# Hybrid trunk on one core: all three branch products walk token tile by token tile, the second tile's inputs are finished late, and the skip multiply of the state space branch changes engine

## The chip, the cores and the metric

The kernel runs on one core of one Trainium2 chip. The time is device microseconds of one execution; several runs are taken and their median is given. A profiled execution has a time of its own and a span, from its first to its last instruction.

## What is computed

Two layers over 256 tokens of 1024 channels. A layer is a feed-forward block, a mixer and a second feed-forward block. Only the mixer is touched. From the reference:

```python
q, k, v, z, xbc, dt_raw, u, vg, gate_raw = jnp.split(xn @ w_in, split_at, axis=-1)
y_a = moba_attention(q, k, v)                        # 8 heads of 128, causal, ALiBi
xbc = jax.nn.silu(causal_depthwise_conv(xbc, conv_w, conv_b))
xs, bm, cm = jnp.split(xbc, ...)
y_s = ssd_scan(xs, dt, a, bm, cm) + d_skip[:, None] * xs     # the skip: d_skip * xs
y_s = rms_norm(y_s * jax.nn.silu(z), ssm_norm_g)
y_c = u * sv                                         # gated unit from u and vg
merged = gates[0]*(y_a @ p_attn) + gates[1]*(y_s @ p_ssm) + gates[2]*(y_c @ p_sgu)
return merged @ w_out
```

## The kernel before, in words

The 256 tokens are two token tiles of 128 (t = 0 and 1); TensorE (PE) multiplies them by weights that arrive as blocks of 128 x 1024 (`raw`, one 512 KB DMA each, issued on SyncE's queue, SP). Every product is taken in split precision: ScalarE (ACT) casts a block to `whi` (L180), VectorE (DVE) subtracts to get `wlo` (L181), and PE runs three matmuls of 512 columns for each unit of 128 input channels: `whi`, `wlo` with the high part of the activations, `whi` with the low part (L213, L214, L215). A block serves two units of each token tile. Eleven split blocks (`SPLIT`) and six raw ones (`RAW`) can be held.

The order of every engine's instructions is written by the program itself. Side work is a Python generator, a task: `spawn` puts it on a list, and after each unit `pump(0.65)` lets 0.65 of planned time pass and steps those whose delay is over. `yield W["pv"]` means that the task goes on 13.0 planned units later; `finish(task)` steps it to its end at once. So the delays in the table `W` decide between which units of a weight product the instructions of a task are written, and each engine runs its own list in that order.

`gemm(..., tail=8)` takes the last eight blocks by token tile: all 16 units of t = 0 (48 matmuls), then all 16 of t = 1. With `tail=0` the tiles alternate, two units of one and two of the other.

The mixer's order is: projections xbc, z, q, k, v; meanwhile the state space task `ssd`; then for each branch its gate projection and its branch product `br`. Branch 0 is the state space branch (input `ysx`), branch 1 attention (`yax`), branch 2 the gated unit (`ycx`, which already has `tail=8`). Between branches 0 and 1 stands the projection vg.

The names that the argument uses:
- `ssd`: for each tile t and group g (of 2), PE makes `seg` (L707), DVE and ACT turn it into weights `ssw` (L709, L713 on ACT, L715; two halves), PE multiplies them with `xs` into `yd` (L738, two halves of eight matmuls), and for t = 1 also `yo` (L744). DVE adds `yd` to `y` (L741), which frees one of the three psum slots `tr` for the next `seg`; then L746, L748, L749. The skip product (L695) puts d_skip * xs into `y` before that. L698 scales `xs` by dt in place.
- `y` is then transposed through memory (L277 on DVE, `turn<-y` and `y<-turn` on SP) and split into `ysh` and `ysl` (ACT L674, DVE L675), the inputs of branch 0; `yt` holds one such task for each tile.
- `qtok` transposes (L277) belong to the q and k tiles.
- `attention`: scores `qk` (L798), DVE adds the position term into `sc` (L802), maximum (L807), `nmx` (L809), exponentials on ACT (L814), division (L820), transposes through memory (L277, `turn<-sc` x8, then `sc<-turn` x2), and `W["pv"]` later the products `pv` (L837) on PE, whose results are split into `yah` and `yal` for branch 1.
- `merge` (L916 and below): DVE multiplies a finished `br` tile by its gate.

Of the kernel before, what the change touches and what calls it, by code (L numbers as in the profile page):

```python
# [16 lines left out]
P = 128  # L17
# [7 lines left out]
NH = 8  # L25
# [26 lines left out]
def trunk(ctx, tc, a):  # L52
# [31 lines left out]
    def tr(name):  # L84
        return psum.tile([P, 512], F32, name=name, tag="tr", bufs=TR)

    def small(name, n, dt=F32, bufs=2):
        return sm.tile([P, n], dt, name=name, tag=name, bufs=bufs)
# [187 lines left out]
    def turn(src, m, e=128):  # L276
        V.transpose(src, src)  # L277
        rd = dram.tile([m, 4, 32, 4, e], F32, name=f"turn{m}_{e}", tag=f"turn{m}_{e}", bufs=8)
        for b in range(4):
            nc.sync.dma_start(rd[:, :, :, b, :].rearrange("m c i e -> i (m c) e"),  # L280
                              src[32 * b:32 * b + 32].rearrange("p (x e) -> p x e", e=e))
        return rd

    def land(dst, rd):
        nc.sync.dma_start(dst, rd.rearrange("m c i a e -> (c i) m (a e)"))
# [202 lines left out]
    def mixer(l, x, r2, nxt):  # L488
# [189 lines left out]
        def ssd(ysx, rs):  # L678
# [13 lines left out]
            def scaled(t):  # L692

                y[t] = b4(f"y{t}")
                G.tensor_tensor(h3(y[t]), h3(xs[t]), hpar[:, l, 2, :, None].to_broadcast([P, SH, SP]),  # L695
                                op=ALU.mult)
                xdt[t] = xs[t]
                V.tensor_tensor(h3(xdt[t]), h3(xs[t]),  # L698
                                st["dt"][:, t * SH:(t + 1) * SH, None].to_broadcast([P, SH, SP]), op=ALU.mult)
# [19 lines left out]
            for t in range(NT):  # L719
                for g in range(SG):  # L720
                    weights(t, 2 * g)
                    if t == 0:
                        scaled(g)
                    yield W["w1"]
                    weights(t, 2 * g + 1)
                    if t == 0:

                        pst = tr("state")
                        T.matmul(pst, bc["b"][:, g * P:(g + 1) * P], xw[:, 512 * g:512 * g + 512],
                                 start=True, stop=True)  # L730
                        A.copy(state[:, 512 * g:512 * g + 512], pst)
                    yield W["w2"]
                    c = slice(512 * g, 512 * g + 512)
                    py = tr("yd")
                    for q in (2 * g, 2 * g + 1):
                        for j in range(4):
                            hh = q * 4 + j
                            T.matmul(py[:, (hh - 8 * g) * SP:(hh - 8 * g + 1) * SP], ws[t, q][:, j, :],  # L738
                                     xdt[t][:, hh * SP:(hh + 1) * SP], start=True, stop=True)
                        ws.pop((t, q))  # L740
                    V.tensor_tensor(y[t][:, c], py, y[t][:, c], op=ALU.add)  # L741
                    if t == 1:
                        po = tr("yo")
                        T.matmul(po, cT(g, 1), state[:, c], start=True, stop=True)  # L744
                        tmp = b2("yo")
                        V.tensor_tensor(h3(tmp, 8), h3(po, 8),  # L746
                                        st["eac"][:, 8 * g:8 * g + 8, None].to_broadcast([P, 8, SP]), op=ALU.mult)
                        V.tensor_tensor(y[t][:, c], y[t][:, c], tmp, op=ALU.add)  # L748
                    V.tensor_tensor(y[t][:, c], y[t][:, c], zs[t][:, c], op=ALU.mult)  # L749
                rs[t] = rsqrt([sumsq(y[t], "sy")], "rs", 1.0 / D)  # L750
                yt[t] = spawn(turned(t, y[t], pl[:, G_SSM:G_SSM + 8]), wait=1.3 if t else 6.5)
# [26 lines left out]
                A.activation(vv[t][:, 512 * c:512 * c + 512], ps[t], AF.Copy, scale=r2[t])  # L778
            yield W["vv"]

        def attention(yax, free):
            for t in range(NT):
                while t and not free:
                    yield 0

                m = t + 1
                n = m * P
                per = 512 // n
                sc, s4 = {}, {}
                mx = small("mx", NH)  # L790
                for g in range(2):
                    sc[g] = (b4 if t else b2)("sc", (P, 4 * n))
                    s4[g] = sc[g].rearrange("p (b h j) -> p h b j", h=4, j=32)
                    for u in range(0, 4, per):
                        ps = tr("qk")
                        for j in range(per):
                            hh = u + j
                            T.matmul(ps[:, j * n:(j + 1) * n], qk["q", g][:, hh, t * P:(t + 1) * P],  # L798
                                     qk["k", g][:, hh, 0:n // 32], start=True, stop=True)
                        for j in range(per):  # L800
                            hh = u + j
                            V.scalar_tensor_tensor(s4[g][:, hh], alibi[t].rearrange("p (b j) -> p b j", j=32),  # L802
                                                   2.0 ** -(4 * g + hh + 1),
                                                   ps[:, j * n:(j + 1) * n].rearrange("p (b j) -> p b j", j=32),
                                                   op0=ALU.mult, op1=ALU.add)
                        yield W["qs"]
                    V.tensor_reduce(mx[:, 4 * g:4 * g + 4], s4[g], axis=AX.XY, op=ALU.max)  # L807
                nmx = small("nmx", NH)
                V.tensor_scalar(nmx, mx, -1.0, None, op0=ALU.mult)  # L809
                den = small("den", NH)  # L810
                for g in range(2):
                    for j in range(4):
                        c = slice(4 * g + j, 4 * g + j + 1)
                        A.activation(s4[g][:, j], s4[g][:, j], AF.Exp, bias=nmx[:, c], accum_out=den[:, c])  # L814
                    yield W["ex"]
                rden = small("rden", NH)
                V.reciprocal(rden, den)
                rd = {}
                for g in range(2):
                    V.tensor_tensor(sc[g].rearrange("p (b h j) -> p b h j", h=4, j=32),  # L820
                                    sc[g].rearrange("p (b h j) -> p b h j", h=4, j=32),
                                    rden[:, None, 4 * g:4 * g + 4, None].to_broadcast([P, 4 * m, 4, 32]), op=ALU.mult)
                    rd[g] = turn(sc[g], m)
                    yield 1.3
                yield W["so"]
                for g in range(2):
                    land(sc[g].rearrange("p (m e) -> p m e", m=m), rd[g])
                yield W["pv"]
                hi, lo = yax.new(t)
                for g in range(2):  # L830

                    pts = sc[g].rearrange("p (m a h j) -> p m h a j", m=m, a=4, h=4)
                    po = tr("pv")
                    for j in range(4):
                        hh = 4 * g + j
                        for k in range(t + 1):
                            T.matmul(po[:, j * P:(j + 1) * P], vv[k][:, hh * HD:(hh + 1) * HD], pts[:, k, j],  # L837
                                     start=k == 0, stop=k == t)
                    halves(po, hi[:, 4 * g:4 * g + 4, :], lo[:, 4 * g:4 * g + 4, :])
                    yield 1.3  # L840


        uu, vg = {}, {}
# [78 lines left out]
                yield W["mg"]  # L922
                yield from to_parts(merged[t], *then.new(t))

        def branch(bx, rs, need, first=False, then=None):
            store = {}
            es = []
            for c in range(2):
                [ps] = project("gate")
                es.append(spawn(gate_evac(store, c, ps, rs)))  # L930
            finish(*need)
            finish(*es)
            slots, dst = accs("br")
            ready, out = set(), {}

            def on_done(key, t):
                ready.add((key, t))
                if t not in out:
                    out[t] = spawn(merge(t, slots, ready, store, first, then))

            gemm(chunk(0) + chunk(1), bx.h, bx.l, dst, tail=8 if then is not None else 0, on_done=on_done)
            return out

        ysx, yax, ycx, mx = XT("ys"), XT("ya"), XT("yc"), XT("mg")
# [17 lines left out]
        finish(ss)  # L962
        finish(*at)
        free = []
        att = spawn(attention(yax, free))
        b0 = branch(ysx, rs, [ss, *yt.values()], first=True)
        free.append(True)
        gl = []
        for c in range(2):
            gl.append(spawn(gelu_evac(vg, "vg", c, project("vg")[0])))  # L970
        b1 = branch(yax, None, [att, *b0.values()])
        gw = spawn(spatial_weights(l))
        finish(*gl)
        gl = [spawn(gelu_evac(uu, "u", 0, project("u")[0]))]
# [204 lines left out]
```

## Time and profile before

| | |
|---|---|
| median of 3 runs | 1488.76 us (1488.53 to 1488.9) |
| profiled execution, its own time | 1487.31 us |
| profiled execution, span | 1485.5 us |
| outside the span | 1.81 us |
| PE busy | 1458.3 us, 98% of the span |
| DVE, ACT, GpSimd (POOL) busy | 970.1, 767.6, 57.0 us |
| granted TensorE clock, mean | 0.997 |

The profiled execution lies 1.45 us below the median. A time in a row is counted from the start of the span; an instruction's duration includes overlap with the next one, so the distance between two starts says what it costs. What stands in brackets behind a row is the idle time of the engine ahead of it and what ended it.

### The profile page before, as it was taken

How to read it: one execution, taken by the hardware profiler on the slowest of the kernel's cores; microseconds unless marked ns; L12 is line 12 of the kernel's file. 1: busy time of each engine (PE TensorE's matmuls, PEld its weight loads, DVE VectorE, ACT ScalarE, POOL GpSimd, SP SyncE). 2: the span in 40 equal slices, each digit the busy share in tenths (PEclk: the TensorE clock that was granted, in tenths of full speed). 3: DMA queues.
4: the chain of work that ended last, by engine and by line, in shares of the span. 5: the costliest groups of instructions: out<-in, count | busy, mean ns of one | idle time of the engine just before them, and what ended most of it. 6: DMA issues, size and time to landing. Idle time of an engine off the chain costs nothing.

```text
span 1485.5 us, 18564 instructions
## 1 busy us (share of the span) xinstructions
PE 1458.3 (98%) x6706; PEld 1204.4 (81%) x6706; DVE 970.1 (65%) x1188; ACT 767.6 (52%) x1051; POOL 57.0 (4%) x98
## 2 busy tenths in 40 slices
PE   9999999999989999999999999999999899999998
PEld 6888888777878888888888888888778788888886
DVE  6766477777666857666486564876776667676652
ACT  6544367555464537544364443765553644464441
POOL 0000021000000001000000000210000000000000
PEclk9999999999999999999999999999999999999999
DMA  8977655577567445877458874656774765477860
GB/s 291 333 227 255 198 185 183 156 201 246 190 216 228 167 155 197 284 242 255 154 193 281 252 254 128 217 169 172 250 230 155 232 206 170 136 265 245 260 200 28
DMA packets 151003, 312.23 MB, mean 210 GB/s; under 512 B 35456, under 2 KB 76544, under 8 KB 150912
## 3 DMA queue, kind: packets, MB, share of 16 engines
q1 hardware_dynamic: 150336, 310.73, 64.6%
q8 instruction: 52, 0.85, 0.2%
q10 hardware_dynamic: 576, 0.33, 0.1%
q14 instruction: 39, 0.32, 0.1%
HBM read 288.98 MB, written 22.02 MB: 209 GB/s over the span
## 4 chain that ended last, share of the span: by engine, by line
PE 61%; DVE 9%; ACT 3%; DMA 3%; issue 2%; POOL 0%; SPq 0%; DVEq 0%; ACTq 0%; POOLq 0%
PE gu L213 8%; PE gu L215 8%; PE gu L214 8%; DVE wlo L181 5%; PE dn L213 4%; PE dn L215 4%; PE dn L214 4%; PE br L213 3%; PE br L215 3%; PE br L214 3%; ACT whi L180 1%; PE wo L213 1%; PE wo L215 1%; PE u L215 1%; PE u L214 1%
## 5 line engine op out<-in xcount | busy, mean ns | idle before, releaser
L181 DVE TENSOR_TENSOR wlo<-raw,whi 128x1024 fp32r<-128x1024 f32 x495 | 595.3, 1225 | 330.1 <-ACT whi L180 329.5
L180 ACT CAST whi<-raw 128x1024 fp32r<-128x1024 f32 x495 | 512.3, 1051 | 404.5 <-PE gu L215 162.8
L213 PE MATMUL gu<-whi,xh 128*128 128x512 f32 x704 | 276.0, 392 | 1.9 <-ACT xh L328 1.5
L214 PE MATMUL gu<-wlo,xh 128*128 128x512 f32 x704 | 274.9, 390 | 0.0
L215 PE MATMUL gu<-whi,xl 128*128 128x512 f32 x704 | 274.6, 390 | 0.0
L213 PEld LDWEIGHTS gu<-whi,xh 128*128 128x128 f32 x704 | 132.5, 188 | 30.2 <-ACT xh L328 2.0
L215 PEld LDWEIGHTS gu<-whi,xl 128*128 128x128 f32 x704 | 132.5, 188 | 28.2 <-DVE xl L329 0.6
L214 PEld LDWEIGHTS gu<-wlo,xh 128*128 128x128 f32 x704 | 132.5, 188 | 28.2 <-DVE wlo L169 0.9
L213 PE MATMUL dn<-whi,hTh 128*128 128x512 f32 x352 | 137.5, 391 | 0.0
L215 PE MATMUL dn<-whi,hTl 128*128 128x512 f32 x352 | 137.0, 389 | 0.0
L214 PE MATMUL dn<-wlo,hTh 128*128 128x512 f32 x352 | 136.9, 389 | 0.0
L215 PEld LDWEIGHTS dn<-whi,hTl 128*128 128x128 f32 x352 | 66.1, 188 | 13.9
L214 PEld LDWEIGHTS dn<-wlo,hTh 128*128 128x128 f32 x352 | 66.1, 188 | 13.5
L213 PEld LDWEIGHTS dn<-whi,hTh 128*128 128x128 f32 x352 | 66.1, 188 | 13.3
L213 PE MATMUL gate<-whi,xh 128*128 128x512 f32 x192 | 76.6, 399 | 0.0
L215 PE MATMUL gate<-whi,xl 128*128 128x512 f32 x192 | 74.9, 390 | 0.0
L214 PE MATMUL gate<-wlo,xh 128*128 128x512 f32 x192 | 74.8, 389 | 0.0
L328 ACT CAST xh<-xg 128x512 fp32r<-128x512 f32 (+1 forms) x25 | 15.1, 603 | 62.1 <-DVE xg L326 62.1
L713 ACT ACTIVATE ssw<-ssw,nacs 128x128 f32<-128x128 f32 x64 | 20.5, 390 | 49.6 <-DVE ssw L709 49.6
L215 PEld LDWEIGHTS gate<-whi,xl 128*128 128x128 f32 x192 | 36.0, 188 | 7.7
L214 PEld LDWEIGHTS gate<-wlo,xh 128*128 128x128 f32 x192 | 36.1, 188 | 6.9
L417 ACT ACTIVATE silu<-gu,r 128x512 f32<-128x512 f32 (+1 forms) x48 | 31.4, 654 | 19.9 <-PE gu L215 16.2
(239 smaller groups left out, 2229.3 us busy)
## 6 DMA issues: line engine op xcount, KB each, us to landing
raw<-in_mix SPq DMA_DIRECT2D x232, 512.0 KB, 4.4
raw<-in_gu SPq DMA_DIRECT2D x175, 512.0 KB, 4.9
raw<-in_dn SPq DMA_DIRECT2D x88, 512.0 KB, 4.5
turn<-hh SPq DMA_DIRECT2D x160, 64.0 KB, 1.8
hh<-turn SPq DMA_DIRECT2D x40, 256.0 KB, 5.3
row_ffn_post_g<-in_ffn_post_g SPq DMA_DIRECT2D x4, 512.0 KB, 5.2
turnw<-qtok SPq DMA_DIRECT2D x32, 64.0 KB, 2.6
qT<-turnw SPq DMA_DIRECT2D x4, 512.0 KB, 6.1
```

The costliest lines, as they stand in the source:

```text
L180: A.copy(hi, w)
L181: V.tensor_tensor(lo, w, hi.bitcast(F32), op=ALU.subtract)
L213: T.matmul(o, xh(k, t), hi[:, off:off + n], start=first, stop=False)
L214: T.matmul(o, xh(k, t), lo[:, off:off + n], start=False, stop=False)
L215: T.matmul(o, xl(k, t), hi[:, off:off + n], start=False, stop=last)
L328: A.copy(o_h, xg)
L417: A.activation(silu[t][:, :w], gate(t), AF.Silu, scale=r2[t])
L713: A.activation(w[:, j, :], w[:, j, :], AF.Exp, bias=st["nacs"][:, c:c + 1])
```

## The change

Four edits. The skip product L695 is taken by DVE, where GpSimd took it. The delay ahead of the second half of a group in `ssd` grows by 1.3 planned units for t = 1. `attention` becomes one task for each tile, and its delay ahead of `pv` grows from 13.0 to 19.5 for t = 1. `branch` always uses `tail=8`, and can finish the tasks of a tile (`late`) when the product first asks for that tile, instead of finishing all of them ahead of the product: branch 0 does so with `yt`, branch 1 with the attention tasks. (The body of `attention` is otherwise only indented less and is cut here.)

```diff
-                G.tensor_tensor(h3(y[t]), h3(xs[t]), hpar[:, l, 2, :, None].to_broadcast([P, SH, SP]),
+                V.tensor_tensor(h3(y[t]), h3(xs[t]), hpar[:, l, 2, :, None].to_broadcast([P, SH, SP]),
                                 op=ALU.mult)
...
-                    yield W["w2"]
+                    yield W["w2"] + 1.3 * t
...
-        def attention(yax, free):
-            for t in range(NT):
-                while t and not free:
-                    yield 0
+        def attention(t, yax, free):
+            while t and not free:
+                yield 0
...
-                yield W["pv"]
+            yield W["pv"] + 6.5 * t
...
-        def branch(bx, rs, need, first=False, then=None):
+        def branch(bx, rs, need, late=None, first=False, then=None):
...
-            gemm(chunk(0) + chunk(1), bx.h, bx.l, dst, tail=8 if then is not None else 0, on_done=on_done)
+
+            if late is not None:
+                bx = guarded(bx, gate_on(late, finish))
+            gemm(chunk(0) + chunk(1), bx.h, bx.l, dst, tail=8, on_done=on_done)
...
-        att = spawn(attention(yax, free))
-        b0 = branch(ysx, rs, [ss, *yt.values()], first=True)
+        att = {t: spawn(attention(t, yax, free)) for t in range(NT)}
+        b0 = branch(ysx, rs, [ss], yt, first=True)
+        finish(att[0])
         free.append(True)
...
-        b1 = branch(yax, None, [att, *b0.values()])
+        b1 = branch(yax, None, [*b0.values()], att)
```

The helper that finishes a tile's task when the product first asks for it was there before:

```python
def gate_on(tail, finish):
    seen = set()
    def wait(k, t):
        if t not in seen:
            finish(tail[t])
            seen.add(t)
    return wait
```

How instructions move, in layer 1 (layer 2 moves in the same way). First DVE, in the state space task of tile 1 (`y_2583`) while the v projection runs on PE; the transposes of a k tile (`qtok`) are the row that moves:

```order
 L277 STREAM_TRANSPOSE y_2468<-y_2468 128x1024
 L181 TENSOR_TENSOR wlo<-raw,whi 128x1024
+L277 STREAM_TRANSPOSE qtok<-qtok 128x512 x2
 L741 TENSOR_TENSOR y_2583<-yd,y_2583 128x512
 L746 TENSOR_TENSOR yo<-yo,eac 128x512
```

They now stand ahead of the L741 that frees the psum slot; before they stood six rows further on, behind the next L715. The two skip products stand on DVE directly ahead of each L698, and a group's `yd` of tile 1 is written six matmuls later on PE (group 0) and twelve later (group 1).

Second PE, the start of branch product 0 (`ysh_3023`, `ysl_3024` are tile 0, `ysh_3198` and `ysl_3199` tile 1):

```order
-L213 MATMUL br<-whi,ysh_3198 128x512
-L214 MATMUL br<-wlo,ysh_3198 128x512
-L215 MATMUL br<-whi,ysl_3199 128x512
-L213 MATMUL br<-whi,ysh_3198 128x512
-L214 MATMUL br<-wlo,ysh_3198 128x512
-L215 MATMUL br<-whi,ysl_3199 128x512
 L213 MATMUL br<-whi,ysh_3023 128x512
 L214 MATMUL br<-wlo,ysh_3023 128x512
```

The units of tile 1 are gone from between those of tile 0: 48 matmuls of tile 0 now stand ahead of the first of tile 1, where six did. The `pv` of attention tile 0 keeps its place, 24 matmuls behind the start of the product.

Third PE, the first `pv` of attention tile 1, inside the gate projection of branch 1 (`xh0`, `xh1` are the two token tiles, the number behind `whi` is that of the block). Before it stood ahead of block 3456:

```order
L837 MATMUL pv_3714<-sc_3438,v1_2928 128x128
L213 MATMUL gate_3648<-whi_3456,xh0_1595 128x512
L214 MATMUL gate_3648<-wlo_3457,xh0_1595 128x512
```

Now it stands ahead of the second tile's units of block 3516:

```order
L836 MATMUL pv_3768<-sc_3438,v1_2928 128x128
L213 MATMUL gate_3747<-whi_3516,xh1_1682 128x512
L214 MATMUL gate_3747<-wlo_3517,xh1_1682 128x512
```

That is 30 matmuls of 512 columns later. On SP the read `y<-turn` of tile 1 stands behind one more `raw` load than before; no other load of the mixer passes another.

## Rows read from the trace of the kernel before

**Rows 1.** Head of the page: the span, and PE's busy time.
```profile
span 1485.5 us, 18564 instructions
PE 1458.3 (98%) x6706; PEld 1204.4 (81%) x6706; DVE 970.1 (65%) x1188; ACT 767.6 (52%) x1051; POOL 57.0 (4%) x98
```

**Rows 2.** Waits of PE, whole execution: releaser, us in total, times, longest.
```profile
PE pv L837 <- DMA sc<-turn: 8.3, 2, 4.2
PE yd L738 <- DVE ssw L715: 4.7, 4, 1.4
PE br L213 <- ACT ysh L674: 3.1, 2, 1.6
```

**Rows 3.** PE in order of time, layer 1, state space task beside the v projection.
```profile
301.04 1.89 PE L738 MATMUL yd<-xs,ssw 128*128 128x64 f32 x16
...
314.19 1.00 PE L738 MATMUL yd<-xs,ssw 128*128 128x64 f32 x8
316.64 1.10 PE L738 MATMUL yd<-xs,ssw 128*128 128x64 f32 x8 [1.45 <-DVE ssw L715]
...
322.10 0.50 PE L707 MATMUL seg<-acsr,sel 128*128 128x512 f32 x1 [0.47 <-DVE y L741]
...
332.50 1.10 PE L738 MATMUL yd<-xs,ssw 128*128 128x64 f32 x8 [0.90 <-DVE ssw L715]
```

**Rows 4.** PE in order of time, layer 1, branch product 0.
```profile
365.72 0.39 PE L214 MATMUL br<-wlo,ysh 128*128 128x512 f32 x1
365.95 0.39 PE L215 MATMUL br<-whi,ysl 128*128 128x512 f32 x1
367.88 0.50 PE L213 MATMUL br<-whi,ysh 128*128 128x512 f32 x1 [1.55 <-ACT ysh L674]
...
372.37 1.05 PE L837 MATMUL pv<-sc,v 128*128 128x128 f32 x8
```

**Rows 5.** PE in order of time, layer 1, the two pv sets of attention tile 1.
```profile
428.28 3.50 PE L837 MATMUL pv<-sc,v 128*128 128x128 f32 x16 [4.09 <-DMA sc<-turn]
...
433.01 1.95 PE L837 MATMUL pv<-sc,v 128*128 128x128 f32 x16
```

**Rows 6.** Stretches: PE, PEld, DVE, ACT, POOL busy, granted clock, DMA share, GB/s.
```profile
240.00:290.00 50.00, 50.00 (x269) 41.42 (x268) 32.92 (x56) 29.45 (x46) 4.41 (x2) 1.00 0.56 168
...
415.00:440.00 25.00, 20.91 (x102) 17.88 (x101) 18.11 (x20) 16.79 (x23) 0.00 (x0) 0.93 0.79 250
```

**Rows 7.** GpSimd (POOL) in order of time, 240 to 260 us.
```profile
248.16 1.91 POOL L695 TENSOR_TENSOR y<-xs,hpar 128x1024 f32<-128x1024 f32 x1 [25.54 <-DMA raw<-in_mix]
250.41 2.50 POOL L695 TENSOR_TENSOR y<-xs,hpar 128x1024 f32<-128x1024 f32 x1 [0.35 <-ACT xs L563]
```

**Rows 8.** DVE in order of time, layer 1, state space task.
```profile
290.02 1.23 DVE L181 TENSOR_TENSOR wlo<-raw,whi 128x1024 fp32r<-128x1024 f32 x1 [2.65 <-ACT whi L180]
...
295.12 1.22 DVE L698 TENSOR_TENSOR xs<-xs,dt 128x1024 f32<-128x1024 f32 x1
...
300.61 0.69 DVE L715 TENSOR_TENSOR ssw<-ssw,cbt 128x512 f32<-128x512 f32 x1 [1.35 <-ACT ssw L713]
...
321.37 0.68 DVE L741 TENSOR_TENSOR y<-yd,y 128x512 f32<-128x512 f32 x1
...
327.34 1.30 DVE L277 STREAM_TRANSPOSE qtok<-qtok 128x512 f32<-128x512 f32 x2
...
331.75 0.69 DVE L715 TENSOR_TENSOR ssw<-ssw,cbt 128x512 f32<-128x512 f32 x1 [1.41 <-ACT ssw L713]
```

**Rows 9.** SP's DMA issues in order of time, layer 1.
```profile
365.91 0.89 SPq L285 DMA_DIRECT2D sc<-turn  x2
...
423.61 0.93 SPq L285 DMA_DIRECT2D sc<-turn  x2
```

**Rows 10.** DMA issues of 340 to 440 us: KB each, median us to landing.
```profile
sc<-turn SPq DMA_DIRECT2D x2, 256.0 KB, 5.2
```

**Rows 11.** DVE in order of time, layer 1, the merges of branch product 0.
```profile
389.15 1.29 DVE L916 TENSOR_TENSOR merged<-br,gate 128x512 f32<-128x512 f32 x2 [9.46 <-PE br L214]
```

More of the change, by code (lines that the diff above doesn't have):

```diff
@@ L779, in v_evac @@
             yield W["vv"]
-        def attention(yax, free):
-            for t in range(NT):
-                while t and not free:
-                    yield 0
[L786 to L827, printed above, removed]
-                yield W["pv"]
[L829 to L840, printed above, removed]
@@ new lines, in attention @@
+        def attention(t, yax, free):
+            while t and not free:
+                yield 0
+            m = t + 1
+            n = m * P
+            per = 512 // n
+            sc, s4 = {}, {}
+            mx = small("mx", NH)
+            for g in range(2):
+                sc[g] = (b4 if t else b2)("sc", (P, 4 * n))
+                s4[g] = sc[g].rearrange("p (b h j) -> p h b j", h=4, j=32)
+                for u in range(0, 4, per):
+                    ps = tr("qk")
+                    for j in range(per):
+                        hh = u + j
+                        T.matmul(ps[:, j * n:(j + 1) * n], qk["q", g][:, hh, t * P:(t + 1) * P],
+                                 qk["k", g][:, hh, 0:n // 32], start=True, stop=True)
+                    for j in range(per):
+                        hh = u + j
+                        V.scalar_tensor_tensor(s4[g][:, hh], alibi[t].rearrange("p (b j) -> p b j", j=32),
+                                               2.0 ** -(4 * g + hh + 1),
+                                               ps[:, j * n:(j + 1) * n].rearrange("p (b j) -> p b j", j=32),
+                                               op0=ALU.mult, op1=ALU.add)
+                    yield W["qs"]
+                V.tensor_reduce(mx[:, 4 * g:4 * g + 4], s4[g], axis=AX.XY, op=ALU.max)
+            nmx = small("nmx", NH)
+            V.tensor_scalar(nmx, mx, -1.0, None, op0=ALU.mult)
+            den = small("den", NH)
+            for g in range(2):
+                for j in range(4):
+                    c = slice(4 * g + j, 4 * g + j + 1)
+                    A.activation(s4[g][:, j], s4[g][:, j], AF.Exp, bias=nmx[:, c], accum_out=den[:, c])
+                yield W["ex"]
+            rden = small("rden", NH)
+            V.reciprocal(rden, den)
+            rd = {}
+            for g in range(2):
+                V.tensor_tensor(sc[g].rearrange("p (b h j) -> p b h j", h=4, j=32),
+                                sc[g].rearrange("p (b h j) -> p b h j", h=4, j=32),
+                                rden[:, None, 4 * g:4 * g + 4, None].to_broadcast([P, 4 * m, 4, 32]), op=ALU.mult)
+                rd[g] = turn(sc[g], m)
+                yield 1.3
+            yield W["so"]
+            for g in range(2):
+                land(sc[g].rearrange("p (m e) -> p m e", m=m), rd[g])
+            yield W["pv"] + 6.5 * t
+            hi, lo = yax.new(t)
+            for g in range(2):
+                pts = sc[g].rearrange("p (m a h j) -> p m h a j", m=m, a=4, h=4)
+                po = tr("pv")
+                for j in range(4):
+                    hh = 4 * g + j
+                    for k in range(t + 1):
+                        T.matmul(po[:, j * P:(j + 1) * P], vv[k][:, hh * HD:(hh + 1) * HD], pts[:, k, j],
+                                 start=k == 0, stop=k == t)
+                halves(po, hi[:, 4 * g:4 * g + 4, :], lo[:, 4 * g:4 * g + 4, :])
+                yield 1.3
```

## The prediction

> **What bounds the kernel now.** I read the head of the page first: PE is busy for 1458.3 of 1485.5 us [rows 1], so all that a change of order can return lies in the 27.2 us that PE stands, plus what it loses at a lower clock. The list of PE's waits says where: 8.3 us for the transposed attention scores of tile 1, 4.7 us for the state space weights, 3.1 us for the second tile's input of branch product 0 [rows 2]. Each comes twice or four times, so once or twice in each layer, and I work through layer 1. In time order PE waits 1.45, 0.47 and 0.90 us in the state space task [rows 3], 1.55 us in branch product 0 [rows 4], 4.09 us at the first `pv` of tile 1 [rows 5]. That is 8.46 us a layer. A sixth loss is no wait: the first `pv` set of 16 matmuls, right behind those 4.09 us, took 3.50 us, the second one 1.95 [rows 5], and the granted clock of that stretch is 0.93 where 240 to 290 us shows 1.00 [rows 6]. So 1.55 us went to the lower of the clock's two levels. With it a layer loses 10.0 us, two layers 20.0: the most that the change could return.
>
> As a measure of distance on PE I use the start to start of two matmuls of 512 columns, 365.72 to 365.95, 0.23 us [rows 4]: six are 1.4 us, 12 are 2.8, 30 are 6.9, 48 are 11.0.
>
> **The skip product.** GpSimd loses two instructions of 1.91 and 2.50 us [rows 7]. Nothing waits for them: PE is busy for all 50.00 us of 240 to 290 [rows 6]. DVE gains two. The trace has no L695 on DVE; the nearest row is L698, also two operands of 128x1024 in float32, at 1.22 us [rows 8]; the bounds are that and POOL's 2.50. I take 1.2. The one of tile 0 is absorbed, because DVE waits 2.65 us for ACT before 290.02 [rows 8]. The one of tile 1 stands ahead of L698 at 295.12; behind it DVE and ACT pass the `seg` weights back and forth (L715 at 300.61 waits 1.35 us only for ACT [rows 8], and ACT for DVE), so nothing takes the delay up. L715 ends at 300.61 + 0.69 = 301.3 and would end at 302.5. PE asks for that half at 301.04 + half of 1.89 = 302.0 [rows 3]: **a new wait of 0.5 us**, and the DVE chain stays 1.2 us later.
>
> **`yd` of tile 1, group 0.** PE comes to it 1.4 us (six matmuls) + 0.5 us later, its weights 1.2 us later: 1.45 + 1.2 - 1.9 = **0.75 us** in place of 1.45.
>
> **`seg` behind it.** It needs the psum slot that L741 at 321.37 frees. L741 is later by the 1.2 us of the chain and by the two `qtok` transposes that now stand ahead of it, 1.30 us [rows 8]: 2.5 us. PE comes 1.4 + 0.5 - 0.7 = 1.2 us later. The wait grows from 0.47 to **1.8 us**.
>
> **`yd` of tile 1, group 1.** Its last L715 ended at 331.75 + 0.69 = 332.4; it is up to 2.5 us later, less the 1.30 us of transposes that stood at 327.34 and have been done: 333.6 [rows 8]. PE asked at 332.50 - 0.90 = 331.6 [rows 3] and now asks 2.8 us (12 matmuls) + 0.5 - 0.7 + 1.3 later, at 335.5. **No wait**, by 1.9 us. The state space part thus waits 0.5 + 0.75 + 1.8 = 3.05 us where it waited 2.82: **+0.2 us**.
>
> **Branch product 0.** Tile 1's input, for which PE waited until 367.88, is asked for 48 matmuls behind the start instead of six, some 9.6 us later: the 1.55 us go. What is late next is `pv` of tile 0, 24 matmuls behind the start in both orders. PE reached it at 372.37 without waiting [rows 4], but only because it had lost 1.55 us before. Its scores were asked for on SP at 365.91 [rows 9] and such a read takes 5.2 us [rows 10], the second of the two up to 0.9 longer: 371.1 to 372.0. In the new order the scores follow the state space task's DVE work, later by at most those 1.2 to 2.5 us. I choose 0.8 to 1.0, since transposes through memory and a wait for ACT lie between, which leave room: 372.0 to 373.0. PE comes at 372.37 - 1.55 + 0.2 = 371.0, or at 370.6 if the slow matmuls behind the old wait go too: a new wait of 1.0 to 2.4, and I take **1.6 us**. So this part returns -1.55 + 1.6 = **0**.
>
> [...] The trace: 1.55 us of waiting left the clock as it was, while 4.09 us was followed by 1.55 us lost at the lower level [rows 4 to 6]. [...]
>
> **`pv` of tile 1.** The read of its scores was issued at 423.61 [rows 9], and PE could start at 428.28 [rows 5]. It now comes 30 matmuls later: 428.28 - 4.09 = 424.2, + 6.9 + 0.2 = 431.3. If the scores were no earlier at all, they would land 3.0 us ahead of PE; the wait and its slow set go: **-5.64 us**. Earlier in the chain DVE stood 9.46 us for the merge at 389.15 [rows 11], since both tiles of the product ended together; tile by tile it merges tile 0 in the middle of the product, so the scores are more likely earlier than later. What is covered: the attention results are asked for only at branch 1's second tile.
>
> **Sum.** A layer: +0.2 + 0 - 5.64 = -5.4 us; layer 2 has the same waits [rows 2], so -10.9 us. On the profiled execution's own 1487.31 that is 1476.4, and with the 1.45 us by which the median lies above it **1478 us**.
>
> **The rivals.**
> - *Everything returns.* The transposes and the skip hide better than I walked, no wait takes the place of the old ones: 20.0 us, 1468.8 us. For it: DVE is busy for 970.1 of 1485.5 us only [rows 1]. Against: in the stretch that matters the chain is DVE and ACT in turns, without a gap behind 295.12 that takes up 1.2 us.
> - *The gain is given back earlier.* Skip at POOL's 2.50 us, `seg` waits 3 us, tile 0's `pv` 3 us and perhaps at the lower clock: +1.3 +1.2 +1.4 +1.5 = 5.4 us a layer more than the sum, which then is 0. Half of it gives 1483.5, all of it 1489. The case that the change does nothing lies here. For it: all three waits hang on the one DVE chain.
> - *Slower: PE starves for split blocks.* In a tile pass PE uses a block each six matmuls, 1.4 us, where alternating it took 2.8. A block costs DVE 1.23 us [rows 8]; eight are 9.8 us of the 11.0 of a pass, and the second tile's input (L673, L675, twice each), two gates, one result and one merge add eight instructions of 128x512, at the 0.69 us of L715 [rows 8] another 5.5. Its place is the first pass of branch products 0 and 1, its price up to 15.3 - 11.0 = 4.3 us for each, 8.6 a layer, +17.2: with the sum, 1495 us. It decides from 5.4 us a layer on, that is, if fewer than two of the eight blocks are split ahead. Against it: eleven are held, and DVE's 9.46 us [rows 11] are time in which it had no free place to split into.
>
> **How the numbers follow.** No change and change part at about 0.2%, 3 us, so at 1485.8 and 1491.7. Chances: my forecast (1472 to 1481.5) 0.57; everything returns 0.10; given back 0.24, of it 0.12 below 1485.8 and 0.10 within 3 us and 0.02 above; starved 0.09, of it 0.07 slower. So faster 0.79, same 0.12, slower 0.09. The forecast's own bounds come from tile 0's `pv` (1.0 to 2.4), the skip (1.22 to 2.50) and `seg`. The range goes from 1471 to 1487: what it leaves out is half of the first rival, a part of the second and most of the third.
>
> **What would show it.** PE's list of waits should have lost `pv` <- `sc` of 4 us for tile 1 and the `br` <- `ysh` row, and have instead `seg` <- `y` L741 of some 1.8 us and a `pv` of tile 0 near 371 us of 1 to 2.4 us; `yd` waits 0.5 and 0.75 and none at group 1 of tile 1; the first `pv` set of tile 1 takes about 1.95 us, and its stretch shows a clock of 1.00. L695 on DVE shows 1.2 us. I am wrong if `br` or `vg` waits for `wlo`, if tile 1's `pv` still waits, or if the wait at tile 0's `pv` is 3 us or more.

## The result, and the profile after

The changed kernel takes 1475.97 us (median of 4 runs, 1475.18 to 1476.04), the kernel before 1488.64 (4 runs on the same chip): a ratio of 0.9915, interval 0.9898 to 0.9932, 12.7 us less. The forecast was 1478 us. The profiled execution takes 1475.94 us, its span is 1473.8. One of the five executions of number 9 below, the profiled one, took 2014.18 us, with a granted clock of 0.16 to 0.18 from 1350 us on, and is left out of its time.

The list of PE's waits (releaser, us in total, times, longest):

```profile
PE seg L707 <- DVE y L741: 3.5, 2, 1.8
PE pv L836 <- DMA sc<-turn: 3.0, 2, 1.5
PE yd L738 <- DVE ssw L715: 2.1, 4, 0.6
PE sv L881 <- DVE ycl L322: 1.5, 2, 1.2
```

Against [rows 2]: the `ysh` row is gone, `pv` has fallen from 8.3 to 3.0 us, `yd` from 4.7 to 2.1, `seg` has come up, and `sv`, a product of the gated unit, is new. The places, PE in order of time in layer 1:

```profile
302.25 1.10 PE L738 MATMUL yd<-xs,ssw 128*128 128x64 f32 x8 [0.57 <-DVE ssw L715]
...
317.48 1.10 PE L738 MATMUL yd<-xs,ssw 128*128 128x64 f32 x8 [0.49 <-DVE ssw L715]
...
324.23 0.47 PE L707 MATMUL seg<-acsr,sel 128*128 128x512 f32 x1 [1.75 <-DVE y L741]
...
334.08 1.89 PE L738 MATMUL yd<-xs,ssw 128*128 128x64 f32 x16
...
371.57 1.13 PE L836 MATMUL pv<-sc,v 128*128 128x128 f32 x8 [1.51 <-DMA sc<-turn]
...
430.11 1.95 PE L836 MATMUL pv<-sc,v 128*128 128x128 f32 x16
...
433.28 1.95 PE L836 MATMUL pv<-sc,v 128*128 128x128 f32 x16
```

Read beside [rows 3 to 5], this is the forecast's list. Three waits in the state space task, 0.57 + 0.49 + 1.75 = 2.81 us, where there were 1.45 + 0.47 + 0.90 = 2.82; none at group 1 of tile 1. The wait in the branch product has gone over to `pv` of tile 0, 1.51 us for 1.55. Both sets of tile 1 take 1.95 us, without a wait, and the clock of that stretch is whole (same columns as [rows 6]):

```profile
415.00:440.00 25.00, 25.00 (x128) 21.28 (x127) 18.90 (x21) 18.73 (x25) 0.00 (x0) 1.00 0.83 272
```

VectorE's rows show the causes. The skip product takes the 1.22 us that were assumed, and the two `qtok` transposes stand ahead of the L741 for which `seg` waits:

```profile
294.76 1.22 DVE L695 TENSOR_TENSOR y<-xs,hpar 128x1024 f32<-128x1024 f32 x1
...
322.21 1.29 DVE L277 STREAM_TRANSPOSE qtok<-qtok 128x512 f32<-128x512 f32 x2
323.43 0.65 DVE L741 TENSOR_TENSOR y<-yd,y 128x512 f32<-128x512 f32 x1
```

In layer 1 the second `pv` set starts at 433.28 where it started at 433.01, with 30 more matmuls (6.8 us) done by then, and the layer's first `state` product (L729) 0.37 us earlier (277.02 in place of 277.39; that difference comes from the start of the program). So up to there the mixer of layer 1 returned 6.8 - 0.27 - 0.37 = 6.2 us; layer 2 comes out at the same 6.2.

The wait at `sv`, in VectorE's and PE's order of layer 2:

```profile
1202.16 1.23 DVE L483 TENSOR_TENSOR wsp<-wsp,con 128x1024 f32<-128x1024 f32 x1 [1.52 <-DMA wsp<-in_sgw]
...
1235.11 1.28 DVE L322 SCALAR_TENSOR_TENSOR ycl<-xtr,ych 128x512 fp32r<-128x512 f32 x2
```
```profile
1235.85 1.16 PE L881 MATMUL sv<-vg,wsp 128*128 128x128 f32 x8 [1.23 <-DVE ycl L322]
```

VectorE comes to the mask of the spatial weights (L483) 1.52 us before their load lands, and everything behind it, down to the `ycl` that `sv` needs, is late. Before the change it did not wait there:

```profile
1213.37 1.22 DVE L483 TENSOR_TENSOR wsp<-wsp,con 128x1024 f32<-128x1024 f32 x1
```

The load's issue on SP, then its KB and us to landing, then the 8 us ahead of the issue (columns as in [rows 6]), before the change:

```profile
1206.76 0.43 SPq L480 DMA_DIRECT2D wsp<-in_sgw  x1
```
```profile
wsp<-in_sgw SPq DMA_DIRECT2D x1, 512.0 KB, 5.0
```
```profile
1198.00:1206.00 8.00, 8.00 (x37) 6.61 (x36) 5.81 (x7) 3.00 (x4) 0.00 (x0) 1.00 0.70 215
```

And after it:

```profile
1194.42 0.43 SPq L480 DMA_DIRECT2D wsp<-in_sgw  x1
```
```profile
wsp<-in_sgw SPq DMA_DIRECT2D x1, 512.0 KB, 7.7
```
```profile
1186.00:1194.00 8.00, 8.00 (x37) 6.63 (x36) 7.93 (x10) 5.28 (x5) 0.00 (x0) 1.00 0.94 293
```

So the load was issued 12.3 us earlier, almost as much as PE had gained, but took 2.7 us longer; the busy share of the DMA engines ahead of it was 0.94 in place of 0.70. The tile order lies behind this. A block is given free at its last unit, so the eight blocks of a tile pass are held until the second tile's pass: from 1175 to 1181 us nothing is loaded (0 GB/s), and then SP issues a block every 1.4 us (eight in 11.38 us) where it issued one every 2.5 (seven in 17.71). In the four versions whose branch product 1 alternates (before, numbers 1, 5 and 10) this load takes 4.8 to 5.4 us and VectorE does not wait for it; in all others it takes 5.9 to 8.3. Number 10 differs from number 8 in the tile order alone: 4.9 to 5.3 us against 6.7 to 7.2.

PE was 12.8 us ahead of the kernel before at the third of the four `sv` sets of layer 2 (1232.17 for 1244.98) and is 11.7 ahead at the fourth (1235.85 for 1247.54): 1.1 us given back. In layer 1 the same wait is 0.31 us, and 0.2 us are given back. The span is 11.7 us shorter.

### The profile page after: what moved, and what is told of

It is laid out like the page before. It is cut to its first block, busy times and chain, and to the rows that moved or that the text cites. A ratio compares the mean times of both kernels' runs of the same rounds, so it can differ in the third digit from the quotient of the medians.

```text
span 1473.8 us, 18560 instructions
## 1 busy us (share of the span) xinstructions
PE 1454.1 (99%) x6706; PEld 1202.5 (82%) x6706; DVE 973.5 (66%) x1192; ACT 767.7 (52%) x1051; POOL 48.1 (3%) x94
## 4 chain that ended last, share of the span: by engine, by line
PE 90%; DVE 5%; ACT 2%; DMA 1%; issue 1%; POOL 0%; SPq 0%; DVEq 0%; ACTq 0%; POOLq 0%
PE gu L213 11%; PE gu L215 11%; PE gu L214 11%; PE dn L214 5%; PE dn L215 5%; PE dn L213 5%; PE br L213 3%; PE br L215 3%; PE br L214 3%; DVE wlo L181 2%; PE gate L213 2%; PE gate L214 2%; PE gate L215 2%; PE xbc L213 1%; PE xbc L215 1%; PE xbc L214 1%
```

## The experiments

**Theory A** is the prediction's account: PE waits for chains that pass through VectorE; moving `pv` of tile 1 behind its scores returns most; the skip on VectorE costs 1.2 us of chain a layer; tile order and `yd` delay move waits. Its rivals: **B**, the tile order does it, by making the scores earlier; **C**, the scores have a pace of their own, so that what is saved ahead of them is waited for at `pv` of tile 0; **D**, the tile order is worth nothing. Up to four versions ran beside the kernel before, on one chip each time; times of different groups are compared by their ratio to it.

**1. Only the later `pv`, on the kernel before.**

```diff
-                yield W["pv"]
+                yield W["pv"] + 6.5 * t
```

> The kernel before with only the later pv of attention tile 1 (the delay of 13.0 becomes 19.5 for t = 1). Theory A (the prediction's): the wait of 4.09 us and the 1.55 us at the lower clock go by this alone, 5.6 to 5.8 us a layer, 1477.3 us; PE still waits 1.55 us for ysh in branch product 0, and no pv waits. Rival B (the scores must come earlier, which the tile order does): pv of tile 1 still waits 2 us or more, 1482 us or above.

Measured: 1475.99 us, ratio 0.9919 (0.9904 to 0.9934), so as fast as the whole change. PE's waits:

```profile
PE yd L738 <- DVE ssw L715: 4.6, 4, 1.4
PE br L213 <- ACT ysh L674: 3.1, 2, 1.5
```

No `pv` is in the list, and the other two are those of [rows 2]. A holds, B falls: the scores need not come earlier. Beside this edit, the others together are worth nothing that can be told from zero.

**2. Only the tile order** (branch products by tile, late tasks, attention as two tasks; that is the changed kernel with the skip on GpSimd and without `+ 1.3 * t` and `+ 6.5 * t`).

> The kernel before with only the tile order of branch products 0 and 1, attention as two tasks and the late tasks; skip on GpSimd, both delays as before. Theory A: the ysh wait goes (2.0 us with its slow matmuls), pv of tile 0 waits 1.2 to 1.5 us instead, pv of tile 1 waits about 2.4 us instead of 4.09, as its scores are 2.4 us earlier; the clock stays high behind 2.4 us: 4 us a layer, 1480.5 us; with a fall of the clock 1483.5. Rival B: pv of tile 1 no longer waits and the gain is nearly whole, 1477 us.

Measured: 1482.05 us, ratio 0.9958 (0.9944 to 0.9972). PE in layer 1:

```profile
371.98 1.13 PE L836 MATMUL pv<-sc,v 128*128 128x128 f32 x8 [0.74 <-DMA sc<-turn]
...
426.15 2.91 PE L836 MATMUL pv<-sc,v 128*128 128x128 f32 x16 [2.27 <-DMA sc<-turn]
```

The `ysh` wait is gone and a smaller one stands at `pv` of tile 0; the scores of tile 1 are earlier and `pv` waits 2.27 us where it waited 4.09, near A's 2.4; tile 0 waits 0.74 us where A had 1.2 to 1.5. But the clock fell behind the 2.27 us (0.50 from 428 to 430 us), and the first set took 2.91 us; in layer 2 it took 3.58 us behind a wait of 2.38. A's "the clock stays high" is wrong.

**3. The changed kernel with `pv` early again** (`+ 6.5 * t` taken out).

> The changed kernel with the delay ahead of pv back at 13.0 for t = 1. Theory A: PE asks at 423.3 us, the scores land at 425.8, so pv of tile 1 waits 2.4 us in each layer: 1480.8 us; should the clock fall after that wait, 1484. Rival B: the wait is under 0.5 us and the time 1476 to 1477.

Measured: 1481.84 us, ratio 0.9962 (0.9951 to 0.9973), against 0.9915 of the changed kernel; A's 2.4 us at tile 1 came as 2.50 in layer 1 and 2.09 in layer 2. Layer 1:

```profile
371.98 1.49 PE L836 MATMUL pv<-sc,v 128*128 128x128 f32 x8 [2.12 <-DMA sc<-turn]
375.82 1.15 PE L836 MATMUL pv<-sc,v 128*128 128x128 f32 x8
...
427.95 2.02 PE L836 MATMUL pv<-sc,v 128*128 128x128 f32 x16 [2.50 <-DMA sc<-turn]
```

Here the clock fell behind the wait of 2.12 us (0.50 from 374 to 376 us; 375.82 - 371.98 = 3.84 us where the changed kernel takes 2.35) and not behind that of 2.50 us (1.00 from 428 to 430 us).

**4. The changed kernel with the skip on GpSimd.**

```diff
-                V.tensor_tensor(h3(y[t]), h3(xs[t]), hpar[:, l, 2, :, None].to_broadcast([P, SH, SP]),
+                G.tensor_tensor(h3(y[t]), h3(xs[t]), hpar[:, l, 2, :, None].to_broadcast([P, SH, SP]),
```

> The changed kernel with the skip product back on GpSimd. Theory A: DVE's chain is 1.2 us earlier, the yd waits of 0.57 and 0.49 us go, seg still waits about 1.6 us as PE comes earlier too, pv of tile 0 waits 1.5 us as now: 1.0 us a layer less, 1474 us. Rival C (the chain behind the waits has a pace of its own): what the yd waits return is waited at seg or at pv of tile 0, 1476 us as now.

Measured: 1473.43 us, ratio 0.9902 (0.9879 to 0.9925), 1.9 us less than the changed kernel by the two ratios, 2.5 by the medians, though the intervals overlap. PE, in layer 1, has only these left of the waits of the state space task and `pv`:

```profile
322.98 0.47 PE L707 MATMUL seg<-acsr,sel 128*128 128x512 f32 x1 [1.75 <-DVE y L741]
...
370.43 1.13 PE L836 MATMUL pv<-sc,v 128*128 128x128 f32 x8 [1.63 <-DMA sc<-turn]
```

Both `yd` waits are gone, as A said, and `pv` of tile 0 has not taken them up. The times alone do not decide it; the rows do.

**5. The kernel before with the skip on VectorE**, the counterpart of 4.

> The kernel before with only the skip product on VectorE. Theory A (the 1.2 us on DVE's chain reach PE): yd of tile 0 waits 0.57 us and yd of tile 1 about 2.1 instead of 1.45, so PE is 1.2 us later behind the state space task; the scores are as much later, the waits at ysh and pv stay: 1.0 to 1.2 us a layer, about 2.3 us slower than before. Rival C: the waits behind take it up, no change within 0.5 us.

Measured: 1492.24 us, ratio 1.0023 (1.0014 to 1.0033): slower by 3.4 us by the ratio, 4.2 by the medians. PE in layer 1:

```profile
302.18 1.10 PE L738 MATMUL yd<-xs,ssw 128*128 128x64 f32 x8 [0.55 <-DVE ssw L715]
...
317.41 1.63 PE L738 MATMUL yd<-xs,ssw 128*128 128x64 f32 x8 [1.82 <-DVE ssw L715]
```

The waits are A's in kind, 0.55 us new and 1.82 (A had 2.1) in place of 1.45; over both layers `yd` waits 6.6 us where it waited 4.7. The rest is clock (0.95 from 308 to 340 us, where the kernel before has 1.00): behind the 1.82 us the eight matmuls took 1.63 us in place of 1.10, and PE 3.67 us to the next matmul of the v projection (317.41 to 321.08) in place of 2.08.

**6. The changed kernel with the second k tile's transposes behind L741 again.**

```diff
-            yield 2.6
+            yield 2.6 + (1.3 if which == "k" and c else 0)
```

> The changed kernel with the transposes of the second k tile asked for 1.3 planned units later, so that they stand behind L741 on DVE again. Theory A: seg waits 0.45 us instead of 1.75, and as y, and with it the scores, come 1.3 us earlier too, pv of tile 0 goes on waiting 1.5 us: 1.3 us a layer, 2.6 us less than the changed kernel, 1473.4 us. Rival C: pv of tile 0 waits 2.8 us and the time stays at 1476.

Measured: 1480.75 us, ratio 0.9945 (0.9929 to 0.9961), slower than the changed kernel. PE in layer 1, and `pv` of tile 0 in layer 2:

```profile
322.69 0.49 PE L707 MATMUL seg<-acsr,sel 128*128 128x512 f32 x1 [0.47 <-DVE y L741]
...
343.84 1.13 PE L797 MATMUL qk<-kT,qT 128*128 128x128 f32 x8 [0.62 <-DMA kT<-turn]
...
372.35 1.13 PE L836 MATMUL pv<-sc,v 128*128 128x128 f32 x8 [2.87 <-DMA sc<-turn]
...
1102.40 2.05 PE L836 MATMUL pv<-sc,v 128*128 128x128 f32 x8 [3.45 <-DMA sc<-turn]
1106.81 1.50 PE L836 MATMUL pv<-sc,v 128*128 128x128 f32 x8
```

Of the 1.75 us at `seg`, 1.3 were the transposes, as A said. But `pv` waits 2.87 and 3.45 us, as C said, and in layer 2 PE is slower behind it: 4.41 us from set to set where the changed kernel takes 2.36, with a mean clock of the execution of 0.997 for 0.999. VectorE and SP in layer 1, first in the changed kernel, then here:

```profile
332.20 0.69 DVE L715 TENSOR_TENSOR ssw<-ssw,cbt 128x512 f32<-128x512 f32 x1 [1.35 <-ACT ssw L713]
...
366.70 0.83 SPq L285 DMA_DIRECT2D sc<-turn  x2
```
```profile
329.40 1.30 DVE L277 STREAM_TRANSPOSE qtok<-qtok 128x512 f32<-128x512 f32 x2
...
332.68 0.69 DVE L715 TENSOR_TENSOR ssw<-ssw,cbt 128x512 f32<-128x512 f32 x1 [1.41 <-ACT ssw L713]
...
367.11 0.93 SPq L285 DMA_DIRECT2D sc<-turn  x2
```

The edit moves the transposes within VectorE's list and takes no work out of it. Counted from the layer's first `state` product, which is 0.27 us earlier here, the L741 is 1.2 us earlier (321.95 + 0.27 for 323.43), but the transposes now stand between the last two L715, so the last one is 0.75 us later, and the read of the scores 0.7. In number 4, counted in the same way, the last L715 is 1.2 us earlier (330.95) and the read 1.5 (365.20). In both the scores follow VectorE's chain and have no pace of their own. A's chain holds; A's reading that the scores would gain 1.3 us with L741 is wrong. The late k (0.62 us at `qk`) is a second effect of this edit.

**7. The changed kernel without the 1.3 units ahead of `yd`.**

> The changed kernel without the 1.3 units ahead of yd for t = 1. Theory A: the waits change places; yd of tile 1 waits 1.8 us at group 0 and 1 us at group 1, seg 0.5 in place of 1.75: 3.3 + 0.57 us where it is 2.8 now, 0 to 1 us a layer more, 1476 to 1478 us. Rival (the delay by itself is worth what its matmuls cover, 1.4 us a group): 1478.7 to 1481.

Measured: 1477.57 us, ratio 0.9928 (0.9912 to 0.9943), 1.6 us more by the medians, with overlapping intervals: not decided by the times. The waits of layer 1 are 0.56, 1.83 and 0.87 us at `yd`, and 0.75 at `pv` of tile 0, 4.0 us in all against 4.3 in the changed kernel; the stretch 308 to 340 us has a clock of 0.95. So this edit moves waits, as A said.

**8. Skip on GpSimd, transposes as in 6, `pv` of tile 0 twelve matmuls later.**

```diff
-            yield W["pv"] + 6.5 * t
+            yield W["pv"] + (6.5 if t else 2.6)
```

> The changed kernel with the skip product on GpSimd, the transposes of the second k tile behind L741, and pv of tile 0 twelve matmuls later. Theory A: no yd wait, seg 0.45 us, no wait at either pv: 1.2 + 1.3 + 1.5 us a layer less than the changed kernel, 1468 us. Rival C: the waits go over to another place (sv, or the second tile of a branch product), 1471 us or more.

Measured: 1470.11 us, ratio 0.9878 (0.9863 to 0.9894). No `yd` and no `pv` waits; what is left:

```profile
PE qk L797 <- DMA kT<-turn: 1.6, 2, 0.8
...
PE seg L707 <- DVE y L741: 0.9, 2, 0.5
PE sv L881 <- DVE ycl L322: 0.9, 2, 0.7
```

Of the 2 us short of A, 1.6 are the wait for the late k tile.

**9. The changed kernel with only `pv` of tile 0 later** (the line of 8).

> The changed kernel with only pv of tile 0 twelve matmuls later. Theory A: its wait of 1.5 us goes, 2.7 us of cover are more than it needs, and nothing behind is nearer than 2.9 us: 1.5 us a layer, 1473 us. Rival C: the wait goes over to pv of tile 1 or to the second tile of branch product 0, 1476 us.

Measured: a ratio of 0.9900 (0.9884 to 0.9917), 1472.2 to 1473.78 us in four runs. Up to 1160 us, at a clock of 1.00, the rows of its profiled execution show `pv` of tile 0 and of tile 1 without a wait. A holds in the rows; the intervals of the two ratios overlap.

**10. Number 8 with the branch products alternating again** (`tail=8` back to the old expression).

> The best version so far with branch products 0 and 1 alternating their tiles again. Theory A (the tile order is worth the ysh wait): PE waits 1.5 to 2 us or more for ysh in each layer and some of pv of tile 1's cover is lost: about 4 us more, 1474 us. Rival D (the tile order is worth nothing here): 1470 us.

Measured: 1482.12 us, ratio 0.9960 (0.9946 to 0.9975), 12 us more than number 8. PE in layer 1 and the stretch around it:

```profile
368.98 0.80 PE L213 MATMUL br<-whi,ysh 128*128 128x512 f32 x1 [4.54 <-ACT ysh L674]
```
```profile
365.00:390.00 25.00, 21.02 (x89) 17.38 (x90) 13.38 (x17) 11.56 (x14) 0.00 (x0) 0.86 0.65 219
```

D falls, and A had the size far too small: with the other waits gone PE comes earlier, and the wait for tile 1's input grows to 4.54 us with a fall of the clock behind it (0.86 in this stretch, 1.00 in number 8). Beside the late `pv` alone, the tile order with the 1.3 units is worth 2.6 us by the medians of numbers 1 and 4, whose intervals overlap (the skip on VectorE takes that back in the changed kernel); it is worth 12 us once the state space task no longer holds PE back.

**11. Number 8, but with the last `seg` asked for later in place of the k transposes.**

```diff
-                    yield W["w1"]
+                    yield W["w1"] + (1.3 if t and g else 0)
```

> The best version so far, but in place of the later k transposes the last seg of tile 1 is asked for 1.3 units later. Theory A: seg waits 0.4 us, kT is on time again, the scores have the pace of y0's read, so no pv waits: 1.6 us less than the best version, 1468.5 us. Rival C: the scores are later by the same 1.3 us and pv of tile 0 waits, 1471 us or more.

Measured: 1468.13 us, ratio 0.9867 (0.9852 to 0.9882). `seg` and `qk` no longer wait; `pv` of tile 0 waits 0.83 and 0.90 us.

**12. Number 11 with `pv` of tile 0 six matmuls later again** (2.6 becomes 3.9).

> The last version with pv of tile 0 six matmuls later again. Theory A: the remaining wait of 0.83 and 0.90 us at it goes and none takes its place: 1.7 us less, 1466.4 us, with PE waiting under 0.5 us in each mixer. Rival C: the wait goes over to the input of branch 1, 1468 us.

Measured: 1466.36 us, ratio 0.9856 (0.9839 to 0.9872). It is the fastest median, about 0.6% below the changed kernel by the two ratios; from number 11 it can't be told apart, as the intervals overlap and the profiled spans are 1464.9 and 1465.0 us. PE's whole list:

```profile
PE sv L881 <- DVE ycl L322: 2.6, 2, 1.5
PE warm L1024 <- DVE ones L98: 1.0, 1, 1.0
PE gu L213 <- ACT xh L328: 1.0, 1, 1.0
PE xtr L312 <- DMA h<-in_x: 0.8, 1, 0.8
PE state L729 <- DVE y L741: 0.7, 2, 0.3
```

`pv` no longer waits, but `sv` now waits 2.6 us where it waited 0.5 in number 11. By the rows C is right, though at `sv` and not at branch 1: the load of the spatial weights takes 7.6 and 8.3 us here, and VectorE waits 3.5 us for it.

## Why the prediction came out right, step by step

- **The late `pv`** was the gain: -5.64 us a layer forecast, and number 1 shows it alone to bring the whole ratio. Number 3 shows that taking it out of the change costs 0.0047 of 0.0085 and not all, as the tile order brings the scores earlier and so shortens the same wait. That its data would land ahead of PE even if they came no earlier was the right bound. They did come earlier, by 423.61 - 421.13 = 2.5 us of issue, which was not needed.
- **The skip** took 1.22 us, and its waits were 0.57 at tile 0 (0.5 forecast) and 0.49 at tile 1 (0.75). Number 5 shows it as a loss by its time and its rows, number 4 by its rows. Nothing was gained on GpSimd, as argued from [rows 6, 7].
- **`seg`** waited 1.75 us (1.8 forecast), and number 6 shows 1.3 of them to be the transposes. **`yd` of group 1** waited for nothing, as forecast. The state space task came out at 0 where +0.2 was forecast.
- **Branch product 0**: 1.51 us at `pv` of tile 0 (1.6 forecast) for 1.55 at `ysh`, a zero as forecast. That the size fits so well is in part luck. Counted from the layer's start (0.37 us earlier than before), PE came at 371.57 - 1.51 + 0.37 = 370.4 us (370.6 to 371.0 forecast) and the scores landed at 371.9 (372.0 to 373.0 forecast). Their read went out 1.2 us later (366.70 + 0.37 for 365.91), more than the 0.8 to 1.0 chosen, and took 4.9 us where 5.2 to 6.1 were assumed. The reason for the choice does not hold: the last L715 was 0.8 us later (332.20 + 0.37 for 331.75), and no room behind it took up a delay.
- **The sum**, -5.4 us a layer, measured -6.2. Of the 0.8, 0.2 are the state space task and 0.1 `pv` of tile 0. Some 0.4 are the three matmuls behind the old `ysh` wait, which took from 367.88 to 368.95, 1.07 us in place of 0.69, and were left out of the sum. Against it stands **the step that was missed**: the forecast did not name `sv`, where 0.2 us of layer 1 and 1.1 us of layer 2 were given back: only the order of the loads on SP had been looked at, and not what the tile order does to their pace. In all, the mixers returned 6.2 + 6.2 - 0.2 - 1.1 = 11.1 us for a forecast of 10.9; that the sum fits so well is luck, as the two errors cancel. The profiled execution was put at 1476.4 and came at 1475.94; the 2 us to the median are the 1.45 us added for a profiled execution below its median, which the one after is not.
- **The clock.** The 1.55 us at the lower level behind the old wait of 4.09 us are in the trace before: a granted clock of 0.50 from 428 to 430 us. The forecast put no such loss behind its wait of 1.6 us, from the 1.55 us of the kernel before, behind which the clock is 1.00 (368 to 372 us); after the change it is 1.00 behind the 1.51 us too (372 to 374 us). As a reading of what such waits do this was wrong: see below.
- **The rivals.** "Everything returns" was named at 1468.8 and is reached only by numbers 11 and 12, which have the skip on GpSimd. "Given back earlier" did not come. "Starved for split blocks" did not either: no `br` and no `vg` waits for `wlo` in the list.

## What to carry to other kernels

Ask of each edit what it does alone: here one delay of 6.5 planned units makes the whole 0.85%, and the other edits add nothing to it that can be told from zero, one of them (the skip on the busier engine) being a loss. When PE comes earlier, list what is late next, through to the end of the stage: long runs in an engine's list, where moving work is not removing it (number 6: the transposes out of L741's way, the last L715 0.75 us later), and loads: here the order that holds blocks longer bunched those behind it (eight in 11.38 us in place of seven in 17.71), and the next one took 7.7 us for 5.0. An edit worth 0 to 3 us beside one version can be worth 12 us beside another, so it is to be tried again once the waits ahead of it are gone.

## What the runs showed of the hardware that was not expected

In these runs the granted clock fell behind some short waits of PE and not behind others, and the length of the wait did not tell which. The stretch behind the same `yd` wait of tile 1, first in the kernel before (1.45 us of waiting), then in number 1 (1.43 us); the last three columns are the granted clock, the DMA share and GB/s:

```profile
318.00:320.00 2.00, 2.00 (x9) 1.43 (x8) 2.00 (x3) 1.83 (x3) 0.00 (x0) 1.00 0.75 231
```
```profile
318.00:320.00 2.00, 2.00 (x5) 1.15 (x4) 2.00 (x3) 1.25 (x2) 0.00 (x0) 0.50 0.76 205
```

Five matmul records where there were nine, at a clock of 0.50 in place of 1.00. Waits of 2.12 and 2.27 us (numbers 3 and 2) were followed by 0.50 (374 to 376 and 428 to 430 us), those of 2.50 us (number 3) and 2.87 us (number 6, layer 1) by 1.00 (428 to 430 and 365 to 390 us). Runs of one kernel differ as well: the ten of number 5 have mean clocks from 0.993 to 0.997 and lie between 1490.1 and 1492.9 us. What decides it, no run here shows. A wait on PE cost its length in these runs, or its length and some 1.3 to 2 us more: behind the wait PE took 3.36 us in place of 2.08 in number 1, 3.84 in place of 2.35 in number 3, and 4.41 in place of 2.36 in layer 2 of number 6.
